# A cast moved between two groups of activations, and the last round of a convolution / recurrence loop rewoven

## The chip, the cores and the metric

The kernel runs on one core of a Trainium2 chip. The metric is device time in microseconds (us) for one execution. A core has five engines that run side by side, each with its own in-order queue: TensorE (PE in the profile; PEld is its weight load), VectorE (DVE), ScalarE (ACT), GpSimd (POOL) and SyncE (SP, which here issues nearly all DMA transfers). They wait for one another through semaphores.

## The reference

A two-layer generator backbone over 1024 latent tokens of width 1024 and 256 context tokens, in float32. The change lies in the first layer:

```python
z = h @ p["w_in"]
va, vg, ga, xb, gb = jnp.split(z, ...)             # each 1024 wide
# branch A
u = va * sigmoid(vg)
u = depthwise_conv(u, p["conv_w"], p["conv_b"])    # 31 taps along the tokens
y_a = silu(layernorm(u, ...)) * silu(ga)
# branch B, in both directions along the tokens
u = depthwise_conv(xb, p["sconv_w"], p["sconv_b"]) # 4 taps
r = sigmoid(u @ w_r + b_r); i = sigmoid(u @ w_i + b_i)   # per head of 128 channels
log_a = -8.0 * r * softplus(-lam); a = exp(log_a)
bx = sqrt(-expm1(2.0 * log_a)) * (i * u)
h[t] = a[t] * h[t-1] + bx[t]                       # context tokens first, then latent tokens
y_b = (h_forward + h_backward) * silu(gb)
out = concat([y_a, y_b]) @ p["w_out"]
```

The second layer (multi-scale pooling and a gate) and the final norm follow; the change does not touch them.

## The kernel before

Activations lie transposed: 128 channels on the partitions, tokens along the free dimension, in 8 channel tiles of 1024 tokens (1280 with context). A product in near float32 is made of three matmuls: every operand is split into a high part (`hi`, a cast on ScalarE, line 95) and a low part (`lo = x - hi`, a subtraction, line 96), and `mm3_steps` (line 119) adds hi·hi, hi·lo and lo·hi, 8 contraction steps for each half of 512 tokens. Weights are loaded by DMA and split in the same way by `wload` (line 107): ScalarE makes the high part, POOL the low part, in buffers that exist twice (`wr`, `wh`, `wl`).

**The rounds (lines 522 to 586).** One round for each channel tile j. A round
- takes the product `xb` (made in the round before), applies four taps and gives `uc`, then its high part `uh` (line 538, ScalarE) and its low part `ul` (line 571, VectorE);
- turns the gates of the tile before into decays (`decays`, line 441): for both directions a Tanh, then an Exp, then a Sqrt, in this order on ScalarE by explicit ordering (`issue_after`); the Sqrt's results are called `roots`;
- multiplies the `vg` weights (sigmoid on ScalarE, line 552, ordered behind the last root) and the `va` weights (line 561); VectorE multiplies both to `u` (line 564), which also frees the PSUM tile;
- runs the recurrence of the tile before (`recurrence`, line 460): two products on POOL (lines 463, 465), and for each direction on VectorE one combined product (line 468) and two scans (lines 475, 477); the sum of both directions is stored to DRAM as `yb_raw`;
- multiplies the four gate matrices of this tile (`gate_steps`, line 498, operands `uh` and `ul`), three pieces of tokens each, with a sigmoid on ScalarE (line 511). Between two such gate steps stand two steps of the next round's `xb` product (`weave`, line 515).

The last round has no next `xb`: there the gate steps alternate with the steps of the round's own `va` product:

```python
gws = wload(gw[j], f"gw{j}", nc.gpsimd, n=4 * P) if last else None
...
if last:
    weave(gate_steps(j, gws, (uh, ul), gates), value_steps(), 1)
```

**Behind the rounds.** Lines 716 to 730: for each j the product `gb` (line 722), its Silu (line 726), the product with the stored recurrence (`yr`, line 727), and its split into `ybh` and `ybl`. Then the 31 taps of the convolution, `conv_tap` (line 743), one VectorE instruction per tap and channel tile on a PSUM tile; the sum over channels and the layer norm (lines 771 to 785, the mean by a matmul `mu`, line 773); the output product `wob` of branch B (line 792); and the gate `ga` of branch A (lines 830 to 850), whose product with the normalised `u` is line 838.

**What sets the order.** The text is traced once, and a planner then orders the instructions of each engine by their place in the text and by planned times; a free engine takes the earliest instruction that is ready by the plan. So the taps, which are late in the text, fill VectorE's gaps from the first round on, and the order within each engine's queue is fixed when the kernel is built. `issue_after` adds an ordering on one engine; `high_priority(offset=EVAC)` lifts what empties PSUM. PSUM has four tiles for products (`psum`, 512 tokens) and two wide ones (`wide`: tag `cv` for the convolution, tag `xb` for the `xb` product and every second convolution tile).

Of the kernel before, what the change touches and what calls it, by code (L numbers as in the profile page):

```python
# [15 lines left out]
P = 128  # L16
# [39 lines left out]
def body(ctx, tc, xT, ctxT, cc, ccol, modT, modW, win, gw, wout, wu, grp, wg, wo1, small, edge, ident, outT):  # L56
# [52 lines left out]
    def wload(src, name, eng, n=D, out=None):  # L109
        raw = wpool.tile([P, n], F32, tag="wr", name=f"wr_{name}")  # L110
        load(raw, src)
        if out is None:
            hi = wpool.tile([P, n], F32R, tag="wh", name=f"wh_{name}")
            lo = wpool.tile([P, n], F32R, tag="wl", name=f"wl_{name}")
        else:
            hi, lo = out(f"wh_{name}", F32R), out(f"wl_{name}", F32R)
        split(raw, hi, lo, eng)
        return hi, lo
# [311 lines left out]
    with ExitStack() as actx:  # L430
# [9 lines left out]

        def decays(j, gates):
            rs, roots, last = gates[0::2], [], None

            def after(*args, **kw):
                nonlocal last
                with ExitStack() as octx:
                    if last is not None:
                        octx.enter_context(tc.issue_after(last.ins))
                    last = nc.scalar.activation(*args, **kw)  # L449

            for d in range(2):
                roots.append(ltile(f"th{j}_{d}"))
                after(roots[d], rs[d], AF.Tanh, scale=chalf[:, d * KT + j : d * KT + j + 1])
            for d in range(2):
                after(rs[d], rs[d], AF.Exp, scale=cneg[:, d * KT + j : d * KT + j + 1])
            for d in range(2):
                after(roots[d], roots[d], AF.Sqrt, bias=tiny)
            return roots, last

        def recurrence(j, uc, gates, roots):  # L460
            ats, ius = gates[0::2], gates[1::2]
# [4 lines left out]
            for d in range(2):  # L466
                iu, at = ius[d], ats[d]
                nc.vector.scalar_tensor_tensor(out=iu, in0=at, scalar=1.0, in1=iu, op0=add, op1=mult)
# [8 lines left out]
                nc.vector.tensor_tensor_scan(out=iu[:, lat], data0=at[:, lat], data1=iu[:, lat],  # L477
                                             initial=first, op0=mult, op1=add)
# [34 lines left out]


        def weave(some, others, n):
            for _ in some:
# [9 lines left out]
        for j in range(KT):  # L526
# [10 lines left out]
            uh, ul = utile(f"uh{j}", F32R), utile(f"ul{j}", F32R)  # L537
            nc.scalar.copy(uh, uc)
            taken = []

            roots, root = (None, None) if state is None else decays(j - 1, state[1])
            w = wload(win[KT + j], f"vg{j}", nc.gpsimd)
# [13 lines left out]
            us.append(u)  # L556
            gates, last = [], j == KT - 1

# [6 lines left out]

            gws = wload(gw[j], f"gw{j}", nc.gpsimd, n=4 * P) if last else None
            with ExitStack() as octx:
                if not last:
                    weave((), value_steps(), 1)
                    octx.enter_context(tc.issue_after(taken[0].ins))  # L570
                nc.vector.tensor_tensor(out=ul, in0=uc, in1=uh.bitcast(F32), op=sub)
# [143 lines left out]

    bh, bl = [], []
    for j in range(KT):
        w = wload(win[4 * KT + j], f"gb{j}", nc.gpsimd)
        th, tl = d2tile(f"ybh{j}", F32R), d2tile(f"ybl{j}", F32R)
        for h in range(2):  # L720
            ps = psum(f"gb{j}_{h}")
            mm3(ps, w, (hh, hl), HALF[h])
            y = vtile(f"yr{j}_{h}")
            nc.sync.dma_start(y, yb_raw[j][:, HALF[h]])
            sgt = ttile(f"sb{j}_{h}")
            nc.scalar.activation(sgt, ps, AF.Silu)
            nc.vector.tensor_tensor(out=y, in0=y, in1=sgt, op=mult)
            split(y, th[:, HALF[h]], tl[:, HALF[h]], nc.gpsimd)
        bh.append(th)
        bl.append(tl)  # L730
# [701 lines left out]
```

## Time and profile before

| | us |
|---|---|
| three runs | 1378.43, 1374.39, 1375.69 |
| their median | 1375.69 |
| the profiled execution, whole | 1381.07 |
| its span, first to last instruction | 1379.3 |

The mean granted clock of TensorE over the span is 0.974 of full speed. The profile is that of one execution; times of rows are counted from the first instruction. A row of the timeline has its start, its length, the engine, the line, the operation, the tile written and the tiles read, the shape, how many instructions are merged, and in brackets the idle time of the engine just before it and what ended it. A row of the list of waits has the waiting engine and line, what it waited for, the total, how often and the longest. A row of the busy time by stage has the stage, its length, each engine's busy time with its number of instructions, and the granted clock.

### The profile page before, as it was taken

The numbers are of one execution on the slowest core, as the hardware profiler recorded it, in microseconds if no ns is written. First come the engines' busy times: TensorE is split into PE (matmuls) and PEld (weight loads), VectorE is DVE, ScalarE is ACT, GpSimd is POOL, SyncE is SP. The second block draws the span as 40 slices with busy tenths as digits, with TensorE's granted clock in tenths as the row PEclk, the third lists the DMA queues.
The fourth block names the chain that finished last, engine by engine and source line by source line (L and its number), as shares of the span: only waits on it lengthen the run. The fifth ranks groups of instructions, "written<-read, shape, count | busy, mean of one in ns | idle before, by whom it ended". The sixth has DMA issues, their size and how long they took to land.

```text
span 1379.3 us, 15637 instructions
## 1 busy us (share of the span) xinstructions
PE 1295.9 (94%) x5664; PEld 1048.2 (76%) x5664; DVE 1205.1 (87%) x1587; ACT 632.7 (46%) x906; POOL 363.3 (26%) x182
## 2 busy tenths in 40 slices
PE   7889989898999799999998999999999999999896
PEld 4468868787777587787887887788888888778685
DVE  7998999999999999998778865999999987876775
ACT  6353644674465542304533544754334344634442
POOL 5173534743473555523320004000000000000002
PEclk9899999999999899999999999999999999999997
DMA  9753011111112113343353646424243334758623
GB/s 354 280 180 119 25 59 54 53 40 61 54 35 72 46 46 130 110 151 135 103 185 122 221 154 205 138 93 151 100 145 123 115 115 132 265 190 275 206 107 123
DMA packets 82866, 181.79 MB, mean 132 GB/s; under 512 B 7778, under 2 KB 27618, under 8 KB 82788
## 3 DMA queue, kind: packets, MB, share of 16 engines
q1 hardware_dynamic: 74340, 176.60, 37.8%
q10 hardware_dynamic: 8448, 4.20, 1.0%
q8 instruction: 44, 0.72, 0.2%
q14 instruction: 34, 0.28, 0.1%
HBM read 136.72 MB, written 44.04 MB: 131 GB/s over the span
## 4 chain that ended last, share of the span: by engine, by line
PE 36%; DVE 10%; DMA 7%; issue 2%; ACT 2%; POOL 1%; POOLq 0%; SPq 0%; DVEq 0%; ACTq 0%
PE ga L127 2%; PE ga L128 2%; PE ga L126 2%; PE wob L127 2%; PE wob L128 2%; PE wob L126 2%; DMA wr_g<-wg 1%; DVE ws L986 1%; DMA yr_t<-y_t 1%; DMA wr_v<-wfold 1%; PE qb_g L666 1%; DVE wq_g L96 1%; PE qb_g L669 1%; PE qb_g L668 1%; DVE wq_wo L96 1%
## 5 line engine op out<-in xcount | busy, mean ns | idle before, releaser
L746 DVE SCALAR_TENSOR_TENSOR conv<-u,sm,conv 128x1013 f32<-128x1013 f32 (+14 forms) x232 | 291.2, 1272 | 6.6 <-ACT conv L738 3.8
L1252 POOL TENSOR_TENSOR o<-x,rr 128x256 f32<-128x256 f32 (+1 forms) x9 | 8.0, 923 | 462.9 <-ACT rr L1240 460.0
L511 ACT ACTIVATE g<-g,sm 128x512 f32<-128x512 f32 (+1 forms) x96 | 58.8, 617 | 110.5 <-PE g L510 108.3
L96 POOL TENSOR_TENSOR wl_wu<-wr_wu,wh_wu 128x1024 fp32r<-128x1024 f32 x16 | 39.4, 2470 | 153.9 <-ACT wh_wu L95 147.7
L463 POOL TENSOR_TENSOR g<-g,uc 128x1280 f32<-128x1280 f32 x16 | 47.5, 2967 | 107.9 <-ACT g L511 65.1
L249 PE MATMUL fold<-gh,wh_wu 128*128 128x512 f32 x128 | 53.0, 416 | 5.7 <-ACT wh_wu L95 5.7
L250 PE MATMUL fold<-gl,wh_wu 128*128 128x512 f32 x128 | 52.4, 409 | 3.2 <-DVE gl L96 3.2
L128 PE MATMUL gb<-h0h,wl_gb 128*128 128x512 f32 x128 | 50.7, 398 | 4.8 <-POOL wl_gb L96 4.8
L126 PE MATMUL vg<-h0h,wh_vg 128*128 128x512 f32 x128 | 52.3, 408 | 2.7 <-ACT g L511 2.1
L251 PE MATMUL fold<-gh,wl_wu 128*128 128x512 f32 x128 | 50.7, 405 | 2.3 <-POOL wl_wu L96 2.3
L128 PE MATMUL xb<-h0h,wl_xb 128*128 128x512 f32 x128 | 50.2, 392 | 2.0 <-POOL wl_xb L96 2.0
L127 PE MATMUL wob<-ybl,wh_wob 128*128 128x512 f32 x128 | 50.5, 395 | 1.2 <-POOL ybl L96 1.2
L465 POOL TENSOR_TENSOR g<-g,th 128x1280 f32<-128x1280 f32 x16 | 46.9, 2948 | 16.8 <-ACT th L449 16.8
L127 PE MATMUL vg<-h0l,wh_vg 128*128 128x512 f32 x128 | 51.2, 400 | 0.0
L126 PE MATMUL gb<-h0h,wh_gb 128*128 128x512 f32 x128 | 50.6, 395 | 0.1
L126 PE MATMUL va<-h0h,wh_va 128*128 128x512 f32 x128 | 50.6, 395 | 0.0
L127 PE MATMUL va<-h0l,wh_va 128*128 128x512 f32 x128 | 50.6, 395 | 0.0
L508 PE MATMUL g<-uh,wh_gw 128*128 128x512 f32 (+1 forms) x96 | 36.3, 379 | 15.1 <-ACT wh_gw L95 6.4
L126 PE MATMUL wob<-ybh,wh_wob 128*128 128x512 f32 x128 | 50.6, 396 | 0.0
L128 PE MATMUL wob<-ybh,wl_wob 128*128 128x512 f32 x128 | 49.9, 391 | 0.7 <-POOL wl_wob L96 0.7
L128 PE MATMUL va<-h0h,wl_va 128*128 128x512 f32 x128 | 50.4, 395 | 0.0
L127 PE MATMUL gb<-h0l,wh_gb 128*128 128x512 f32 x128 | 50.4, 393 | 0.0
(548 smaller groups left out, 4301.1 us busy)
## 6 DMA issues: line engine op xcount, KB each, us to landing
mod<-modT SPq DMA_DIRECT2D x28, 512.0 KB, 5.5
wr_wu<-wu SPq DMA_DIRECT2D x16, 512.0 KB, 3.9
x_part<-xp SPq DMA_DIRECT2D x32, 256.0 KB, 2.4
mod<-modT SPq DMA_DIRECT2D x32, 256.0 KB, 3.3
wr_v<-wfold SPq DMA_DIRECT2D x16, 512.0 KB, 3.7
wr_g<-wg SPq DMA_DIRECT2D x16, 512.0 KB, 5.4
wr_wo<-wo SPq DMA_DIRECT2D x16, 512.0 KB, 4.2
yr_t<-y_t SPq DMA_DIRECT2D x16, 512.0 KB, 6.3
```

The lines of the kernel that those rows point to most:

```text
L96: eng.tensor_tensor(out=lo, in0=src, in1=hi.bitcast(F32), op=sub))
L126: nc.tensor.matmul(ps, hi[:, kc], xh[k][:, cols], start=(k == 0), stop=False)
L127: nc.tensor.matmul(ps, hi[:, kc], xl[k][:, cols], start=False, stop=False)
L128: nc.tensor.matmul(ps, lo[:, kc], xh[k][:, cols], start=False, stop=(k == ks - 1))
L249: nc.tensor.matmul(ps, wh[:, kc], gh[i], start=(i == 0), stop=False)
L250: nc.tensor.matmul(ps, wh[:, kc], gl[i], start=False, stop=False)
L251: nc.tensor.matmul(ps, wl[:, kc], gh[i], start=False, stop=(i == 3))
L463: nc.gpsimd.tensor_tensor(out=ius[d], in0=ius[d], in1=uc, op=mult)
L465: nc.gpsimd.tensor_tensor(out=ius[d], in0=ius[d], in1=roots[d], op=mult)
L508: nc.tensor.matmul(ps[:, :n], gwh[:, kc], uh[:, a : a + n], start=True, stop=False)
L511: nc.scalar.activation(t[:, a : a + n], ps[:, :n], AF.Sigmoid, bias=col(ob + d * KT + j))
L746: nc.vector.scalar_tensor_tensor(out=(us[j] if k == 30 else acp)[:, a:b], in0=us[j][:, a + o : b + o], scalar=col(O_CONVW + 31 * j + k), i ...
```

## The change

1. **`decays`** takes an optional pair `cast`; if it is given, the copy `uh <- uc` is put into the ordered series on ScalarE, between the two Exp and the two Sqrt. In the first round, which has no decays, the copy stays alone.
2. **`ul`** follows directly in the text, and no longer waits for the first value tile.
3. **`recurrence`** takes `ahead`: the second direction's product (line 468) is ordered on VectorE behind the second value product.
4. **The last round** loads its gate weights ahead of `vg`, into a buffer of the pool of `uc`, `uh` and `ul`; it makes `va` in one go like the other rounds, and its gate steps alternate, one for one, with the steps of the first `gb` product, which goes to a wide PSUM tile. The Silu of that product stands ahead of the last decays.
5. **The `gb` loop** starts with the second product and asks for each weight tile one tile ahead.
6. `wload` accepts two ready tiles as well as a function that gives them.

```diff
-        def decays(j, gates):
+        def decays(j, gates, cast=None):
 ...
-                    last = nc.scalar.activation(*args, **kw)
+                    last = f(*args, **kw)
 ...
             for d in range(2):
                 after(rs[d], rs[d], AF.Exp, scale=cneg[:, d * KT + j : d * KT + j + 1])
+            if cast is not None:
+                after(*cast, f=nc.scalar.copy)
             for d in range(2):
                 after(roots[d], roots[d], AF.Sqrt, bias=tiny)
 
-        def recurrence(j, uc, gates, roots):
+        def recurrence(j, uc, gates, roots, ahead=None):
 ...
-                nc.vector.scalar_tensor_tensor(out=iu, in0=at, scalar=1.0, in1=iu, op0=add, op1=mult)
+                with ExitStack() as octx:
+                    if d == 1 and ahead is not None:
+                        octx.enter_context(tc.issue_after(ahead.ins))
+                    nc.vector.scalar_tensor_tensor(out=iu, in0=at, scalar=1.0, in1=iu, op0=add, op1=mult)
 ...
+        def project_gate():
+            w = wload(win[4 * KT], "gb0", nc.gpsimd)
+            ps = wide("gb0", 1)
+            return ps, (x for h in range(2) for x in mm3_steps(ps[:, HALF[h]], w, (hh, hl), HALF[h]))
 ...
-            nc.scalar.copy(uh, uc)
+            last = j == KT - 1
             taken = []
-
-            roots, root = (None, None) if state is None else decays(j - 1, state[1])
+            if state is None:
+                nc.scalar.copy(uh, uc)
+                roots, root = None, None
+            else:
+                roots, root = decays(j - 1, state[1], (uh, uc))
+            nc.vector.tensor_tensor(out=ul, in0=uc, in1=uh.bitcast(F32), op=sub)
+            if last:
+                gws = utile(f"gw{j}", F32R)
+                gws = wload(gw[j], f"gw{j}", nc.gpsimd, n=4 * P, out=(gws[:, :H], gws[:, H : 2 * H]))
             w = wload(win[KT + j], f"vg{j}", nc.gpsimd)
 ...
-            gws = wload(gw[j], f"gw{j}", nc.gpsimd, n=4 * P) if last else None
-            with ExitStack() as octx:
-                if not last:
-                    weave((), value_steps(), 1)
-                    octx.enter_context(tc.issue_after(taken[0].ins))
-                nc.vector.tensor_tensor(out=ul, in0=uc, in1=uh.bitcast(F32), op=sub)
-            if last:
-                weave(gate_steps(j, gws, (uh, ul), gates), value_steps(), 1)
+            for _ in value_steps():
+                pass
 ...
-                recurrence(j - 1, *state, roots)
-            if not last:
+                recurrence(j - 1, *state, roots, taken[1])
+            if last:
+                gb0, steps = project_gate()
+            else:
                 xb, steps = project_xb(j + 1)
                 gws = wload(gw[j], f"gw{j}", nc.gpsimd, n=4 * P)
-                weave(gate_steps(j, gws, (uh, ul), gates), steps, 2)
+            weave(gate_steps(j, gws, (uh, ul), gates), steps, 1 if last else 2)
             state = uc, gates
+        sb0 = [ttile(f"sb0_{h}") for h in range(2)]
+        for h in range(2):
+            nc.scalar.activation(sb0[h], gb0[:, HALF[h]], AF.Silu)
         recurrence(KT - 1, *state, decays(KT - 1, state[1])[0])
 ...
     bh, bl = [], []
+    w_next = wload(win[4 * KT + 1], "gb1", nc.gpsimd)
     for j in range(KT):
-        w = wload(win[4 * KT + j], f"gb{j}", nc.gpsimd)
+        w = w_next
+        if 0 < j < KT - 1:
+            w_next = wload(win[4 * KT + j + 1], f"gb{j + 1}", nc.gpsimd)
         th, tl = d2tile(f"ybh{j}", F32R), d2tile(f"ybl{j}", F32R)
         for h in range(2):
-            ps = psum(f"gb{j}_{h}")
-            mm3(ps, w, (hh, hl), HALF[h])
+            if j == 0:
+                sgt = sb0[h]
+            else:
+                ps = psum(f"gb{j}_{h}")
+                mm3(ps, w, (hh, hl), HALF[h])
+                sgt = ttile(f"sb{j}_{h}")
+                nc.scalar.activation(sgt, ps, AF.Silu)
```

More of the change, by code (lines that the diff above doesn't have):

```diff
@@ L114, in wload @@
             lo = wpool.tile([P, n], F32R, tag="wl", name=f"wl_{name}")
+        elif callable(out):
+            hi, lo = out(f"wh_{name}", F32R), out(f"wl_{name}", F32R)
         else:
-            hi, lo = out(f"wh_{name}", F32R), out(f"wl_{name}", F32R)
+            hi, lo = out
         split(raw, hi, lo, eng)
@@ L438, in ltile, with after @@
             return lpool.tile([P, E], dt, tag="l", name=name)
-        def decays(j, gates):
+        def decays(j, gates, cast=None):
             rs, roots, last = gates[0::2], [], None
-            def after(*args, **kw):
+            def after(*args, f=nc.scalar.activation, **kw):
                 nonlocal last
@@ L556, in body @@
             us.append(u)
-            gates, last = [], j == KT - 1
+            gates = []
             def value_steps():
```

2 lines of the change are left out of this document (removed).

## The prediction

> **What bounds the kernel now.** I read the page first, then the chain of work that ended last, then busy time by stage, then who waited for whom inside the stage that the change touches.
>
> ```profile
> span 1379.3 us, 15637 instructions
> PE 1295.9 (94%) x5664; PEld 1048.2 (76%) x5664; DVE 1205.1 (87%) x1587; ACT 632.7 (46%) x906; POOL 363.3 (26%) x182
> ```
>
> TensorE looks like the bound, but a busy PE includes waiting in its pipeline. The chain, from 584 us on, is TensorE without a break, and the first thing on it that is not a `wob` product is the `mu` product of the layer norm:
>
> ```profile
> 584.05 0.50 PE wob L127
> 630.60 0.86 PE mu L773 x2
> ```
>
> The rounds, the `gb` branch and the convolution taps occupy 131 to 629 us:
>
> ```profile
> core 0: us, PE busy (x) PEld busy (x) DVE busy (x) ACT busy (x) POOL busy (x), PEclk, DMA share, GB/s
> 131.00:629.00 498.00, 464.67 (x2086) 380.69 (x2085) 481.99 (x396) 240.41 (x286) 236.81 (x100) 0.97 0.21 69
> 449.00:461.00 12.00, 5.88 (x14) 4.51 (x15) 10.04 (x8) 5.85 (x7) 7.63 (x3) 0.57 0.13 44
> ```
>
> This row decides the case. VectorE is busy 482.0 of 498 us, so it has 16.0 us of idle time in all. Its filler is the 31-tap convolution, which has no deadline inside the rounds but must be complete before `mu`:
>
> ```profile
> L746 DVE SCALAR_TENSOR_TENSOR conv<-u,sm,conv 128x1013 f32<-128x1013 f32 (+14 forms) x232 | 291.2, 1272 | 6.6 <-ACT conv L738 3.8
> ```
>
> So there are two clocks running side by side: TensorE through rounds, `gb` and `wob`, and VectorE through rounds and taps. They meet at `mu`:
>
> ```profile
> 627.95 1.28 DVE L758 TENSOR_TENSOR lnsum<-lnsum,u 128x512 f32<-128x512 f32 x2
> 631.50 9.66 DVE L776 TENSOR_TENSOR u<-u,mu 128x512 f32<-128x512 f32 x16 [1.60 <-PE mu L773]
> ```
>
> The sum over channels ends at 629.2 and `mu` runs at 630.6: today both arrive almost together. After `mu`, VectorE has the whole layer norm to do before it can consume the `ga` products, and TensorE has the rest of `wob` and the first `ga` tiles to do meanwhile. How much room that leaves:
>
> ```profile
> 680.78 1.29 DVE L838 TENSOR_TENSOR u<-u,ga 128x512 f32<-128x512 f32 x2 [0.74 <-ACT ga L836]
> 690.67 0.39 PE L128 MATMUL ga<-h0h,wl_ga 128*128 128x512 f32 x1
> 690.90 0.39 PE L126 MATMUL ga<-h0h,wh_ga 128*128 128x512 f32 x1
> ```
>
> Four PSUM tiles rotate. The second `ga` tile is consumed at 680.78 + 0.65 = 681.4; the sixth, which takes its place, starts at 690.9. TensorE could be 9.5 us earlier relative to VectorE here; beyond that it would stand still.
>
> **The change, part by part.** What TensorE loses today, up to 584 us:
>
> ```profile
> PE g L509 <- DVE ul L571: 6.7, 3, 3.0
> PE g L508 <- ACT wh_gw L95: 6.4, 1, 6.4
> PE g L508 <- DVE u L564: 6.2, 3, 2.3
> PE gb L128 <- POOL wl_gb L96: 4.8, 2, 3.3
> PE xb L128 <- POOL wl_xb L96: 2.0, 2, 1.6
> ```
>
> *TensorE.* `uh` moves ahead of the roots, and `ul` no longer waits for the first value tile, so the 6.7 us on `ul` go. The second direction's `L468` is put behind both value products on VectorE, so these free PSUM sooner and most of the 6.2 us go. In the last round the gate weights are loaded ahead of `vg`, and the value matmuls run first, which covers the 6.4 us. Of the 4.8 us on `wl_gb` I take half, since POOL's order decides it:
>
> ```profile
> 520.86 2.52 POOL L96 TENSOR_TENSOR ybl<-yr,ybh 128x512 fp32r<-128x512 f32 x2 [16.61 <-DMA yb_raw<-g]
> 525.74 0.79 PE L128 MATMUL gb<-h0h,wl_gb 128*128 128x512 f32 x1 [3.30 <-POOL wl_gb L96]
> ```
>
> POOL stood 16.6 us at the first `ybl` until the last recurrence was stored, with the low part of a `gb` weight behind it. Loading a tile ahead helps only where that low part comes before this wait in POOL's order. In all about 21 us. The half-clock stretches behind these waits go too: the stage ran at a mean clock of 0.97, 498 x 0.03 = 15 us lost, and the row 449 to 461 shows how: 0.57 of 12 us, behind the 6.4 us wait, is 5.2 us. Take two thirds of 15: 10. TensorE then reaches `mu` some 25 to 30 us earlier. Alternating the last gates with `gb0` adds no matmul; the matmuls are 0.23 us apart (690.67 and 690.90), so the 12 steps of three that lie between gates hold 8.2 us, and the last gate and with it the last recurrence come that much later in matmul count. Against the 6.4 us wait and its 5.2 us of half clock, that is even or better.
>
> *VectorE.* None of its instructions is removed, so only its waits and slow spots can shrink:
>
> ```profile
> DVE g L468 <- POOL g L465: 5.9, 4, 2.1
> DVE ul L571 <- ACT uh L538: 1.9, 1, 1.9
> DVE yr L727 <- ACT sb L726: 1.6, 1, 1.6
> L571 DVE TENSOR_TENSOR ul<-uc,uh 128x1280 fp32r<-128x1280 f32 x8 | 14.2, 1778 | 1.9 <-ACT uh L538 1.9
> 417.52 1.47 DVE L571 TENSOR_TENSOR ul<-uc,uh 128x1280 fp32r<-128x1280 f32 x1
> 490.73 3.37 DVE L727 TENSOR_TENSOR yr<-yr,sb 128x512 f32<-128x512 f32 x1 [1.59 <-ACT sb L726]
> 526.30 0.68 DVE L727 TENSOR_TENSOR yr<-yr,sb 128x512 f32<-128x512 f32 x1
> ```
>
> `ul` alone takes 1.47 us, its mean is 1.778: 8 x 0.31 = 2.5 us, plus the wait of 1.9, so 4.4 us if it falls where POOL is quiet. The first `yr` product waited 1.6 us for a Silu that now comes before the last decays: 1.6 us. The same product took 3.37 where another took 0.68; I give it half of the 2.7, 1.3 us (bounds 0 and 2.7).
>
> The other side is on ScalarE, and what waits for it:
>
> ```profile
> 397.41 2.62 ACT L449 ACTIVATE th<-th,tiny 128x1280 f32<-128x1280 f32 x2
> 401.35 0.60 ACT L552 ACTIVATE sg<-vg 128x512 f32<-128x512 f32 x1
> 401.84 1.26 ACT L538 CAST uh<-uc 128x1280 fp32r<-128x1280 f32 x1
> 398.92 5.86 POOL L465 TENSOR_TENSOR g<-g,th 128x1280 f32<-128x1280 f32 x2 [1.92 <-ACT th L449]
> 401.91 4.23 DVE L468 SCALAR_TENSOR_TENSOR g<-g,g 128x1280 f32<-128x1280 f32 x1 [1.83 <-POOL g L465]
> ```
>
> The cast (1.26 us, about 1.15 net of overlap) now stands between the exponentials and the roots. Roots, `sg`, POOL's `L465` and VectorE's first `L468` all stand behind it: each comes 1.15 us later in 7 rounds, 8.1 us in all. If `uc` is not finished, the cast and the roots wait for it as well. The cover is `ul` itself, 1.47 us of VectorE work that becomes ready in that gap; where it fills it, the cost is nothing. I take 0, bounds 0 and 8.1. The cast needs no table of its own: in the rows above it follows a sigmoid with no load between.
>
> The wait added to the second direction's `L468` (behind both value products) holds, in VectorE's order, its scans, the sum of both directions and the store of `yb`; the next round's decays take over those buffers.
>
> ```profile
> DVE u L564 <- PE va L128: 1.0, 1, 1.0
> ```
>
> VectorE has waited for a value product once in all rounds, in the first, for 1.0 us; taps stand ready to fill such a gap. I take nothing, bounds 0 and 1.0 per round.
>
> *At `mu`.* If TensorE arrives 25 us early it stands there, with the remaining `wob` tiles queued behind it, and resumes at half clock. By the row 449 to 461 that costs up to 5.2 us; one short stretch is a third of it, 1.7. I take 1.7.
>
> [...]
>
> *No cost on the path:* the new loader form; the last gate weights in the pool of `uc`, whose buffer comes free when POOL has used the previous `uc`, with TensorE on `vg` and `va` meanwhile; one or two table loads around the early Silu. On the SP queue the `gb` weights now stand ahead of the `yr` loads of the same tile; a load that waits for its buffer holds these back, but taps fill VectorE and TensorE has room.
>
> Sum on the path that ends last, VectorE up to `mu` and TensorE after it: -4.4 - 1.6 - 1.3 + 1.7 = **-5.6 us**. The profiled run took 1381.07 us (span 1379.3 plus 1.8 around it), so it would take 1375.5; the median of the runs is 1375.69, 5.4 below the profiled one, so **1370.1 us**.
>
> **Rivals.**
>
> *TensorE's gain gets through.* If the order written for TensorE has `mu` later among `wob` and `ga` tiles, up to 9.5 us more than VectorE's own savings arrives, and nothing is lost to half clock: -7.3 - 9.5 = -16.8 at most, 1359; half the room gives 1364. For it: TensorE has 25 us to give. Against it: the order is fixed at build time from planned times, in which contention and half clock need not appear, so `mu` may keep its place. Chance 0.17.
>
> *POOL's later product runs into the scans: slower.* VectorE and POOL slow one another when both work on SBUF:
>
> ```profile
> 456.76 1.48 DVE L468 SCALAR_TENSOR_TENSOR g<-g,g 128x1280 f32<-128x1280 f32 x1
> 408.91 4.48 DVE L477 TENSOR_TENSOR_SCAN g<-g,g 128x1024 f32<-128x1024 f32 x1
> 465.47 2.32 DVE L477 TENSOR_TENSOR_SCAN g<-g,g 128x1024 f32<-128x1024 f32 x1
> ```
>
> `L468` alone takes 1.48, beside POOL's `L465` 4.23; the scan 2.32 alone and 4.48 where POOL was late. Push `L465` back by 1.15 us in every round and the weight splits behind it land on the scan: 1.15 + 2.16 = 3.3 us per round. In five of seven rounds that is 16.5, less the savings of 7.3 and plus 1.7: +11, so 1387. In four it is +7.6, 1383. It decides from the third round on (9.9 - 7.3 + 1.7 = +4.3). Against it: `ul` fills part of the gap and the second direction is pushed later, where POOL is idle. Chance 0.20, mostly near the lower price.
>
> [...]
>
> *Nothing moves.* VectorE is full, its savings are eaten by the cast or by half clock: within 0.3%, 1376. Chance 0.13.
>
> **How the numbers follow.** The forecast has 0.50: its own spread (cast 0 to 8.1, value wait 0 to 7, `yr` 0 to 2.7, half clock 0 to 5.2) puts 0.33 of it beyond 0.3% and 0.17 within; 0.3% is 4.1 us, about what a measurement of this kernel can tell from no change. Faster: 0.33 + 0.17 = 0.50. Same: 0.17 + 0.13 = 0.30. Slower: 0.20. The range takes in the first rival's full room and the slower one's nearer price: 1358 to 1383.
>
> **What would show it.** Right: the waits for `ul`, `u` and `wh_gw` gone from TensorE's list; rounds shorter; a new wait of TensorE at `mu` or in the first `ga` tiles, 10 us or more; VectorE still busy 97% up to `mu`, which comes about 5 us earlier. Wrong on the fast side: `mu` waits for nobody and `ga` starts 10 us or more earlier. Wrong on the slow side: `L468`, `L475` and `L477` longer than their means now, or a longer wait for `L465`, with `mu` later than 630. The forecast fails altogether if VectorE's idle and slow spots move by more than 10 us for reasons that no row here shows.

## The result, and the profile after

The changed kernel takes **1393.32 us** (median of 4 runs, 1390.43 to 1394.86) against 1377.06 us for the kernel before in the same series: a ratio of 1.0123, 95% interval 1.0101 to 1.0144. It is 16 us slower where 5.6 us less was forecast, and lies above the range. The profiled execution of the changed kernel took 1390.43 us, its fastest; that of before, 1381.07 us, was 4 us above the median. So the two traces differ by 9 us where the medians differ by 16. Runs of one kernel lie up to 7 us to either side of their median: in what follows, sizes come from medians and places from traces.

First the head of the page after: span, and busy time by engine.

```profile
span 1388.6 us, 15640 instructions
PE 1299.9 (94%) x5664; PEld 1048.2 (75%) x5664; DVE 1211.8 (87%) x1587; ACT 637.6 (46%) x910; POOL 364.4 (26%) x182
```

The instructions are the same but for four more on ScalarE. VectorE's take 6.7 us longer in all (1205.1 us before); most of the loss is in waits. The timeline of the changed kernel, at the layer norm and at the first `ga` products:

```profile
641.77 2.78 DVE L784 TENSOR_TENSOR lnsum<-lnsum,u 128x512 f32<-128x512 f32 x1
...
690.77 1.27 DVE L864 TENSOR_TENSOR u<-u,ga 128x512 f32<-128x512 f32 x2
...
691.50 0.79 PE L128 MATMUL ga<-h0h,wh_ga 128*128 128x512 f32 x1 [3.73 <-DVE u L864]
```

The sum over channels ends at 644.6 us, 15 us later than before (629.2). VectorE then starts its `ga` products at 690.8 instead of 680.8, and TensorE, whose first `ga` matmul is on time (664.0 us, 663.5 before), stands 3.7 us in front of them. Of the two rows of busy time by stage below, the first is the whole stage of the prediction and the second the stretch around that wait (columns: length, busy time of TensorE, weight load, VectorE, ScalarE and POOL, granted clock, DMA share, GB/s):

```profile
131.00:629.00 498.00, 463.39 (x2078) 377.57 (x2078) 470.78 (x386) 242.27 (x287) 235.61 (x100) 0.97 0.21 69
...
689.00:697.00 8.00, 5.50 (x14) 4.35 (x15) 4.42 (x8) 8.00 (x9) 2.38 (x1) 0.57 0.07 6
```

VectorE, busy 482.0 us of the stage before, is busy 470.8: it lost 11 us to waiting and has that much work left at 629. Over the 8 us that take in the last 2.5 us of TensorE's wait and what follows it the granted clock is 0.57; the mean of the whole stage is 0.97 as before.

**Two clocks.** A clock means here the time at which one engine, if the other never held it, would bring the last `ga` matmul. All kernels have that matmul as a common point; from there to the end of the span lie 624 to 631 us in every trace. The tile view of before, of the changed kernel, and of the last experiment (which frees two resources) gives a kind of matmul, its count, its shortest, median and longest time in ns, and the first and last start in us:

```profile
L126 PE MATMUL ga<-h0h,wh_ga x128: 388/390/800, 663.5 to 750.3; 128*128 128x512 f32 x128
L128 PE MATMUL ga<-h0h,wl_ga x128: 388/390/398, 664.3 to 750.7; 128*128 128x512 f32 x128
L773 PE MATMUL mu<-lnsum,ones x4: 592/593/593, 630.4 to 632.0; 128*128 128x512 f32 x4
```

```profile
L128 PE MATMUL ga<-h0h,wh_ga x128: 387/389/799, 664.0 to 758.6; 128*128 128x512 f32 x128
L130 PE MATMUL ga<-h0h,wl_ga x128: 388/389/628, 664.5 to 759.0; 128*128 128x512 f32 x128
L799 PE MATMUL mu<-lnsum,ones x4: 590/592/592, 645.5 to 647.7; 128*128 128x512 f32 x4
```

```profile
L128 PE MATMUL ga<-h0h,wh_ga x128: 388/389/398, 652.1 to 739.3; 128*128 128x512 f32 x128
L130 PE MATMUL ga<-h0h,wl_ga x128: 388/389/396, 652.5 to 739.8; 128*128 128x512 f32 x128
L806 PE MATMUL mu<-lnsum,ones x4: 592/592/593, 625.8 to 627.4; 128*128 128x512 f32 x4
```

Where TensorE sets the pace, the last `ga` matmul starts 87.2 us after the first (750.7 - 663.5, before). Where VectorE sets it, it starts 113.5 us after `mu` (759.0 - 645.5, after). These two traces give the two constants; the others test them. The later of the two times meets the last `ga` matmul within 0.7 us in every trace except e2's, where both are close and it is 2 us too high. Some of them:

| kernel | first `ga` + 87.2 | `mu` + 113.5 | last `ga` in the trace |
|---|---|---|---|
| before | 750.7 | 743.9 | 750.7 |
| changed | 751.2 | **759.0** | 759.0 |
| changed, small `gb0` tiles (e3) | 751.8 | 750.7 | 752.3 |
| changed, start of the taps on VectorE (e8) | 759.5 | **770.2** | 770.5 |
| rounds' edits, free memory (e14) | 753.3 | 741.6 | 752.9 |
| changed, free memory (e16) | 747.5 | **755.2** | 755.8 |
| changed, small tiles, free memory (e18) | 739.3 | 739.3 | 739.8 |

Before, VectorE had 6.8 us of room. The change brings TensorE no earlier and VectorE 15 us later; 8.3 us of that shows. That places the 9 us between the two traces; the other 7 us between the medians are a matter of which execution was profiled, and no row here places them.

**Waits that went and came.** TensorE's list of waits after, 131 to 800 us:

```profile
PE gb L128 <- ACT wh_gb L95: 7.8, 2, 4.5
PE g L516 <- DVE uc L548: 7.1, 5, 4.1
...
PE ga L128 <- DVE u L864: 3.7, 1, 3.7
...
PE g L516 <- DVE u L585: 1.6, 3, 0.6
```

The waits for `ul` (6.7) and `wh_gw` (6.4) are gone and most of that for `u`; as much has come elsewhere. On VectorE, 131 to 700 us:

```profile
DVE conv L772 <- ACT conv L764: 9.1, 5, 4.4
DVE yr L753 <- ACT sb L605: 6.4, 1, 6.4
DVE g L476 <- POOL g L470: 5.9, 4, 1.8
```

The wait for the convolution's start has grown from 3.8 to 9.1, that for the first Silu from 1.6 to 6.4; that for POOL's product is what it was.

**The last round.** ScalarE's timeline after, in the last round. Line 519 is the gates' Sigmoid, line 605 the early Silu; line 452 is Tanh where it writes `th` from `g`, Exp where it reads `cneg`, and Sqrt where it reads `tiny`. A table load (`ACT_TABLE_LOAD`, 1.28 us each) is a row with no operands:

```profile
477.06 1.21 ACT L764 ACTIVATE conv<-u,sm 128x1024 f32<-128x1024 f32 x1 [6.68 <-DVE u L778]
478.21 1.03 ACT L519 ACTIVATE g<-g,sm 128x512 f32<-128x512 f32 x2
479.14 1.36 ACT L452 ACTIVATE th<-g,chalf 128x1280 f32<-128x1280 f32 x1
...
482.34 1.28 ACT L452 ACT_TABLE_LOAD   x1
483.64 1.37 ACT L452 ACTIVATE g<-g,cneg 128x1280 f32<-128x1280 f32 x1
485.02 1.28 ACT L519 ACT_TABLE_LOAD   x1
486.32 0.69 ACT L519 ACTIVATE g<-g,sm 128x512 f32<-128x512 f32 x1
487.03 1.28 ACT L452 ACT_TABLE_LOAD   x1
488.32 1.37 ACT L452 ACTIVATE g<-g,cneg 128x1280 f32<-128x1280 f32 x1
...
491.00 2.61 ACT L452 ACTIVATE th<-th,tiny 128x1280 f32<-128x1280 f32 x2
...
494.56 1.28 ACT L605 ACT_TABLE_LOAD   x1
495.86 1.08 ACT L605 ACTIVATE sb<-gb 128x512 f32<-128x512 f32 x2
...
497.31 1.22 ACT L764 ACTIVATE conv<-u,sm 128x1024 f32<-128x1024 f32 x1
```

Three things are to be seen. A convolution's start stands in ScalarE's queue in front of the gates' sigmoids and waits 6.7 us for the previous convolution on VectorE. The last sigmoid then falls between the two exponentials, with a table load of 1.28 us on either side of it (485.02 and 487.03). And the Silu called early runs at 495.9, behind everything; only then is the wide bank free, and the convolution that waits for it starts at 497.3. Before, that convolution started at 452.6, and the two exponentials stood side by side:

```profile
452.63 1.21 ACT L738 ACTIVATE conv<-u,sm 128x1024 f32<-128x1024 f32 x1
...
482.24 2.62 ACT L449 ACTIVATE g<-g,cneg 128x1280 f32<-128x1280 f32 x2
```

For 45 us VectorE had the taps of one convolution to fill its gaps with, instead of two.

**Behind the last recurrence.** After (POOL, then ScalarE):

```profile
525.60 2.54 POOL L96 TENSOR_TENSOR ybl<-yr,ybh 128x512 fp32r<-128x512 f32 x2 [8.69 <-DMA yb_raw<-g]
528.88 0.63 ACT L227 ACTIVATE cH<-cH 128x512 f32<-128x512 f32 x1 [12.98 <-DMA cH<-cc]
```

The first `ybl` belongs to tile 0, whose recurrence was stored long ago; still it waits for the store of the last one. The reason is memory, as e13 to e18 will show: the 16 buffers of `ybh` and `ybl` are laid over those of the rounds, and `ybl` of tile 0 got the buffer of the tile that the last recurrence stores. `cH`, a vector that VectorE first reads at 704 us, lies there too: its load is issued at 525.5, as that store ends.

### The profile page after: what moved, and what is told of

Same layout as the page of the kernel before. It is cut to its first block, busy times and chain, and to the rows that moved or that the text cites. A ratio compares the mean times of both kernels' runs of the same rounds, so it can differ in the third digit from the quotient of the medians.

```text
span 1388.6 us, 15640 instructions
## 1 busy us (share of the span) xinstructions
PE 1299.9 (94%) x5664; PEld 1048.2 (75%) x5664; DVE 1211.8 (87%) x1587; ACT 637.6 (46%) x910; POOL 364.4 (26%) x182
## 4 chain that ended last, share of the span: by engine, by line
PE 39%; DVE 38%; DMA 8%; ACT 6%; issue 6%; POOL 3%; SPq 0%; POOLq 0%; DVEq 0%; ACTq 0%
DVE conv L772 10%; DVE g L476 3%; DVE g L485 2%; DMA yr_t<-y_t 2%; PE wob L128 2%; PE wob L129 2%; PE wob L130 2%; PE fold L253 1%; PE fold L252 1%; PE fold L251 1%; DVE ws L1012 1%; DVE yr L753 1%; DVE uc L548 1%; DVE mod L834 1%; DMA mod<-modT 1%
## 5 line engine op out<-in xcount | busy, mean ns | idle before, releaser
L772 DVE SCALAR_TENSOR_TENSOR conv<-u,sm,conv 128x1021 f32<-128x1021 f32 (+14 forms) x232 | 292.9, 1271 | 11.9 <-ACT conv L764 9.1
L468 POOL TENSOR_TENSOR g<-g,uc 128x1280 f32<-128x1280 f32 x16 | 49.2, 3075 | 84.7 <-ACT g L519 48.3
L128 PE MATMUL ga<-h0h,wh_ga 128*128 128x512 f32 x128 | 51.7, 404 | 3.7 <-DVE u L864 3.7
L130 PE MATMUL vg<-h0h,wl_vg 128*128 128x512 f32 x128 | 50.3, 402 | 1.2 <-POOL wl_vg L96 1.2
L129 PE MATMUL ga<-h0l,wh_ga 128*128 128x512 f32 x128 | 50.8, 397 | 0.0
L130 PE MATMUL ga<-h0h,wl_ga 128*128 128x512 f32 x128 | 50.7, 396 | 0.0
```

Of the source, the lines that this page charges most:

```text
L128: nc.tensor.matmul(ps, hi[:, kc], xh[k][:, cols], start=(k == 0), stop=False)
L129: nc.tensor.matmul(ps, hi[:, kc], xl[k][:, cols], start=False, stop=False)
L130: nc.tensor.matmul(ps, lo[:, kc], xh[k][:, cols], start=False, stop=(k == ks - 1))
L468: nc.gpsimd.tensor_tensor(out=ius[d], in0=ius[d], in1=uc, op=mult)
L772: nc.vector.scalar_tensor_tensor(out=(us[j] if k == 30 else acp)[:, a:b], in0=us[j][:, a + o : b + o], scalar=col(O_CONVW + 31 * j + k), i ...
```

## The experiments

All medians in us; "before" is the kernel before in the same series. The theories in quotation marks are those of the expectations.

### e1 to e4: which half of the change?

e1 keeps the edits of the rounds (cast, `ul`, order of the second direction) and has the last round and the `gb` loop as before; e2 is the reverse. e3 and e4 are the changed kernel with one thing altered:

```diff
 e3
-            ps = wide("gb0", 1)
+                    ps.append(psum(f"gb0_{h}"))
 e4
-                roots, root = decays(j - 1, state[1], (uh, uc))
+            nc.scalar.copy(uh, uc)
+            roots, root = (None, None) if state is None else decays(j - 1, state[1])
```

> The edits of the rounds alone: cast of uh between the exponentials and the roots, ul right behind it, the second direction's L476 behind both value products. The last round and the gb loop stand as before the change. Theory 'last round' (the whole loss comes from gb0 in the wide bank, the convolution that starts late and the late Silu): no loss is left, 3 to 6 us faster than before. Theory 'cast' (the cast holds roots, sigmoids and the convolution's start on ScalarE in each of seven rounds): 8 to 12 us slower than before. Theory 'order' (any edit reshuffles the planned order, each a little worse): both halves slower, 5 to 8 us each.

> The edits of the last round alone: gates alternate with gb0, early gate weights, gb weights a tile ahead, early Silu. The cast, ul and the order of L476 stand as before the change. Theory 'last round': 12 to 16 us slower than before, with convolution 5 starting near 497 us and TensorE waiting 7 us or more on the high part of a gb weight. Theory 'cast': within 4 us of before, or faster. Theory 'order': 5 to 8 us slower.

> The changed kernel with gb0 in two PSUM tiles of 512 tokens, as the other gb products have them, in place of the wide bank that xb and the convolutions' projections take turns in. If the occupied bank is what costs in the last round: convolution 5 starts near 453 us as before the change instead of 497, and the kernel is 8 to 14 us faster than the changed one. If it is ScalarE's order (sigmoids behind the convolution's start, table loads) or the cast: within 3 us of the changed one.

> The changed kernel with the cast of uh as before the change: issued ahead of the decays and free of their order; ul still right behind. Theory 'cast': 5 us or more faster than the changed kernel. Theory 'last round': within 3 us of it.

| | this | before | ratio, interval |
|---|---|---|---|
| e1 rounds alone | 1387.75 | 1377.14 | 1.0062, 1.0040 to 1.0084 |
| e2 last round alone | 1382.49 | 1377.14 | 1.0037, 1.0020 to 1.0053 |
| e3 small `gb0` tiles | 1385.47 | 1377.14 | 1.0052, 1.0032 to 1.0071 |
| e4 cast free | 1393.94 | 1377.14 | 1.0108, 1.0090 to 1.0126 |

Both halves lose, 10.6 and 5.4, and the sum is the whole. The bank is worth 8 of the 16 us: in e3 the convolution that waited for it starts at 455.1 and `mu` comes at 637.2 instead of 645.5. So "last round" explained half; e2 by itself fits the numbers of "order". Theory "cast" had e4 faster by 5 us or more, and it is not. But e4 does not clear the cast, for it pays in another place, in a wait of VectorE that is 1.5 us in the changed kernel:

```profile
DVE ul L556 <- ACT uh L554: 13.1, 5, 4.7
```

How the rounds' edits lose shows in e1, ScalarE first, then POOL, ScalarE and TensorE:

```profile
485.15 0.60 ACT L742 ACTIVATE sb<-gb 128x512 f32<-128x512 f32 x1 [8.20 <-PE gb L130]
...
488.46 1.63 ACT L519 ACTIVATE g<-g,sm 128x256 f32<-128x256 f32 x3 [1.41 <-DVE g L485]
...
533.95 2.51 POOL L96 TENSOR_TENSOR ybl<-yr,ybh 128x512 fp32r<-128x512 f32 x2 [17.05 <-DMA yb_raw<-g]
537.17 0.63 ACT L227 ACTIVATE cH<-cH 128x512 f32<-128x512 f32 x1 [12.09 <-DMA cH<-cc]
540.85 0.79 PE L128 MATMUL gb<-h0h,wh_gb 128*128 128x512 f32 x1 [5.80 <-ACT sb L742]
```

Up to the eighth round TensorE is where it was (its `vg` products start at 436.3; 436.5 before). But the last three sigmoids run at 488.5, the last recurrence is stored 13 us later, ScalarE stands at `cH` with the `gb` Silus behind it, and TensorE runs out of PSUM.

### e5 to e8: which edit of the rounds, and does ScalarE hold the rest?

e5, e6 and e7 are the kernel before with one edit each: `ul` right behind the cast; the second direction's product behind the second value product; the cast between exponentials and roots. e8 is the changed kernel with

```diff
-        nc.scalar.activation(acp, us[j], AF.Identity, bias=col(O_CONVB + j), ...)
+        nc.vector.tensor_scalar(out=acp, in0=us[j], scalar1=col(O_CONVW + 31 * j + 15),
+                                scalar2=col(O_CONVB + j), op0=mult, op1=add)
```

> The kernel before with one edit: ul right behind the cast of uh, no longer behind the first value tile. The edits of the rounds together cost 0.6%, and the cast's place is not the reason in the changed kernel. Theory 'ul first' (1.5 us of VectorE work moves ahead of the convolution's end, whose successor starts on ScalarE in front of the gates' sigmoids): 5 to 10 us slower than before, with ScalarE's waits at the convolution's start near 9 and 7.5 us in place of 5.1 and 3.8. Theory 'order' (any edit reshuffles the planned order): 3 to 5 us slower, and the other two edits as much.

> The kernel before with one edit: the second direction's combined product ordered behind the second value product on VectorE. Theory 'ul first': within 3 us of before. Theory 'second direction late' (its scans and the store come later, and the next decays with them): 5 to 10 us slower. Theory 'order': 3 to 5 us slower.

> The kernel before with one edit: the cast of uh between the exponentials and the roots. Theory 'ul first' and theory 'second direction late': within 3 us of before. Theory 'order': 3 to 5 us slower. Should the cast cost something that the changed kernel hides, 8 us.

> The changed kernel with the convolution's first term (bias and middle tap) made by VectorE instead of ScalarE. No convolution start stands in ScalarE's order then, so it holds no sigmoid, Silu or cast; VectorE gets 8 instructions more, of about 1.2 us each by the taps of the same size, 9.6 us, and loses its own waits for that start (9.1 us). Theory 'ScalarE held by the convolution's start': TensorE's waits behind sigmoids, Silus and casts shrink by half or more, 6 us or more faster than the changed kernel. Theory 'VectorE alone sets the time': within 3 us of the changed kernel, or slower by up to 9.6.

| | this | before | ratio, interval |
|---|---|---|---|
| e5 `ul` alone | 1387.91 | 1376.51 | 1.0082, 1.0061 to 1.0103 |
| e6 order alone | 1382.10 | 1376.51 | 1.0042, 1.0026 to 1.0058 |
| e7 cast alone | 1383.53 | 1376.51 | 1.0053, 1.0036 to 1.0071 |
| e8 start on VectorE | 1400.43 | 1376.51 | 1.0168, 1.0143 to 1.0193 |

Each edit alone loses, and the three lose less together than apart: they lean on one another. The sign that e5's theory named, longer waits at the convolution's start, did not come (VectorE waits 3.8 us for it, as before). e5's are these, of VectorE and of TensorE:

```profile
DVE ul L556 <- ACT uh L554: 23.8, 7, 5.9
```

```profile
PE g L516 <- DVE u L579: 22.2, 6, 5.2
```

Without the cast moved forward, `ul` stands at the head of VectorE's queue and waits for `uh` behind the roots, and the value products that free PSUM wait behind `ul`. e7 is the cast without `ul`:

```profile
DVE g L470 <- POOL g L467: 13.0, 6, 3.3
```

That is 7.1 us more than the 5.9 of before, and the kernel is 7.0 us slower; the prediction put 8.1 us on an uncovered cast. That the one wait makes the whole loss is not shown: by the two clocks e7's later engine is TensorE, whose first `ga` matmul comes 6.5 us later than before (670.0). With `ul` beside the cast the same wait is 5.9 in the changed kernel, 9.0 in e1 and 7.4 in e18, so `ul` covers most of it. e6:

```profile
478.61 0.60 ACT L729 ACTIVATE sb<-gb 128x512 f32<-128x512 f32 x1 [7.80 <-PE gb L128]
...
481.70 1.63 ACT L514 ACTIVATE g<-g,sm 128x256 f32<-128x256 f32 x3 [1.19 <-DVE g L480]
```

In the old last round the value steps alternate with the gates, so "behind the second value product" is late there; the second scan and the buffer that the last gate takes over come late with it (the wait on the scan, line 480 of that kernel). A `gb` Silu planned ahead of these sigmoids holds ScalarE for 7.8 us; the wait that ends last is that for the scan. e8 refutes "ScalarE held by the convolution's start": ScalarE no longer makes that start, but TensorE's first `ga` matmul came 8.3 us later than in the changed kernel (672.3), `mu` at 656.7, and the kernel lost 7 us more. VectorE does not get eight instructions for nothing: the loss is within the 9.6 us that were expected for them.

### e9 to e12: the kernel before once more, and `cH`

e9 is the kernel before. e10 (rounds' edits) and e11 (changed, small tiles) order `cH`'s Silu behind the last `gb` Silu; e12 is e2 with small tiles.

```diff
-        nc.scalar.activation(t, t, AF.Silu)
+            if behind is not None:
+                octx.enter_context(tc.issue_after(behind.ins))
+            nc.scalar.activation(t, t, AF.Silu)
```

> The kernel before, unchanged, profiled once more. Its first profiled execution was 4 us above the median of its runs. Theory 'last recurrence' (the gb product ends 38.7 us after the Silu of the condition vector cH, which waits for the last recurrence's buffer with the gb Silus behind it on ScalarE; in the first profile cH came at 524.2 and left 7.4 us of slack): cH again near 524 and gb's end within 46 us of it; an execution near the median would show 3 to 5 us less half clock or waiting somewhere ahead of 663 us, not a shorter tail.

> The edits of the rounds alone (as in the first experiment), and the Silu of cH ordered on ScalarE behind the last gb Silu; cH is first read near 691 us. Theory 'last recurrence': TensorE's wait behind a gb Silu (5.8 us and the half clock after it) goes, gb ends 5 to 8 us earlier than the 576.1 of the rounds' edits alone, and the time falls by 5 to 10 us, back to within 4 us of before. Theory 'roots late' (what the rounds lose, they lose inside the rounds, by later roots and POOL products): within 3 us of the rounds' edits alone, 1387.8.

> The changed kernel with gb0 in two small PSUM tiles and the Silu of cH behind the last gb Silu. With small tiles alone gb ended at 572.9, 38.6 us after cH, and mu came at 637.2. Theory 'last recurrence': gb ends 4 us or more earlier, but ga is then held by VectorE, 113.6 us from mu to the last ga product: 1 to 3 us faster than small tiles alone (1385.5) by this bound, no more. Theory 'roots late': no change.

> The last round's edits alone (second experiment, 1382.5), with gb0 in two small PSUM tiles. If bank and rounds add up (16.2 = 10.6 for the rounds + 5.4 for the last round, and small tiles take 8 back): 1374 to 1377, no loss against before. If the small tiles only helped beside the rounds' edits: near 1382.

| | this | before | ratio, interval |
|---|---|---|---|
| e9 before again | 1375.50 | 1376.69 | 0.9997, 0.9981 to 1.0013 |
| e10 rounds, `cH` late | 1385.67 | 1376.69 | 1.0062, 1.0041 to 1.0084 |
| e11 small tiles, `cH` late | 1382.19 | 1376.69 | 1.0038, 1.0020 to 1.0056 |
| e12 last round, small tiles | 1384.84 | 1376.69 | 1.0053, 1.0033 to 1.0074 |

e9 repeats the distances of the first trace (the first `ybl` at 518.5 instead of 520.9, the end of `gb` 49.4 us behind it in both) and gives the resolution: 0.2%. e10 gained 2 us where 5 to 10 were expected: the next instruction that waits for the last recurrence has taken `cH`'s place. Its ScalarE:

```profile
541.53 0.62 ACT L95 CAST ybh<-yr 128x512 fp32r<-128x512 f32 x1 [14.43 <-DVE yr L746]
```

TensorE again waits 5.6 us for the `gb` Silu behind it. This `ybh` belongs to tile 1. By the code its `yr` takes one of two buffers, which come free when the first `ybl` is made, and that waits for the store. e11 came out 3.3 us under e3, near the bound of 1 to 3; its trace does not show why, since both `mu` and the last `ga` matmul are 1.4 us later there than in e3's. e12 refutes that bank and rounds add up (8 us above that expectation) and lies nearer the other one, 1382: with the rounds as before, TensorE is the later clock (last `ga` 754.9, `mu` + 113.5 = 747.7), so the bank brings it nothing.

### e13 to e16: the memory freed

Two pools of 8 buffers instead of one of 16; tiles 0 to 3 now lie on memory that is free early. `cH` stays late. e13 is before, e14 the rounds' edits, e15 the changed kernel with small tiles, e16 the changed kernel.

```diff
-    d2pool = ctx.enter_context(tc.tile_pool(name="d2pool", bufs=16, reuse_waits="tile"))
+    d2pools = [ctx.enter_context(tc.tile_pool(name=f"d2pool{i}", bufs=8, reuse_waits="tile")) for i in range(2)]
...
-        return d2pool.tile([P, S], dt, tag="d2", name=name)
+        d2count[0] += 1
+        return d2pools[(d2count[0] - 1) // 8 % 2].tile([P, S], dt, tag="d2", name=name)
```

> The kernel before with two edits. The 16 buffers for ybh and ybl come from two pools of 8 instead of one of 16, so that the tiles of branches 0 to 3 lie on memory that is free by then, and no longer on that of the last recurrence (ybl of tile 0 lay on the buffer whose store ends the last recurrence); and cH's Silu stands behind the last gb Silu. Theory 'buffers of the last recurrence': the 16.6 us of GpSimd at the first ybl and TensorE's 3.3 us at 525 us go, gb ends 3 to 6 us earlier, and since VectorE has 6.7 us of room at ga, the kernel is 3 to 6 us faster than before. Theory 'SP queue' (what stands behind the last store is held by the queue, whatever the memory): within 2 us of before.

> The edits of the rounds alone, with the same two edits. The rounds' edits alone ended gb at 576.1 us, 45.3 us after the last store, with a wait of 5.8 us behind a gb Silu and 6.8 us of half clock; cH alone brought nothing (1385.7), since the casts of ybh took its place. Theory 'buffers of the last recurrence': that wait goes, gb ends near 567, and the time falls 7 to 11 us from 1387.8, to 1377 to 1381. Theory 'roots late' (the loss lies inside the rounds): within 3 us of 1387.8.

> The changed kernel with gb0 in two small PSUM tiles and the same two edits. Theory 'buffers of the last recurrence': gb ends at 562 to 566 instead of 570 to 573; the end then hangs on VectorE, 113.6 us from mu (638 us) to the last ga product: 1380 to 1383, little under the 1382.2 with cH alone. If mu comes earlier as well (the products with the recurrence no longer stand in one heap behind the last store), 1374 to 1379.

> The changed kernel with the same two edits, gb0 still in the wide bank. There mu came at 645.5 and the last ga product 113.5 us later, while TensorE stood before the first of the ga products. Theory 'VectorE sets the end of the changed kernel through the bank': gb ends earlier but the time stays within 3 us of 1393.3. Theory 'buffers of the last recurrence' as the only cause: 7 to 11 us faster.

| | this | before | ratio, interval |
|---|---|---|---|
| e13 before, free memory | 1376.29 | 1377.13 | 0.9991, 0.9976 to 1.0007 |
| e14 rounds, free memory | 1380.47 | 1377.13 | 1.0015, 0.9995 to 1.0035 |
| e15 changed, small tiles, free memory | **1371.98** | 1377.13 | 0.9966, 0.9950 to 0.9983 |
| e16 changed, free memory | 1384.86 | 1377.13 | 1.0054, 1.0033 to 1.0074 |

The rounds' edits lose 7 of their 10.6 us of loss (e14, as expected, though `gb` ends at 572.6 and not near 567), and the changed kernel with both resources free beats the kernel before by 5 us.

Three expectations missed. The kernel before gains nothing from the memory: its `gb` ends at 570.2 as in its first trace. By the time alone that fits the theory "SP queue", but the trace refutes it, since GpSimd no longer waits for the last store, which is issued at 518.6:

```profile
496.73 2.53 POOL L96 TENSOR_TENSOR ybl<-yr,ybh 128x512 fp32r<-128x512 f32 x1
```

The wait went, and the end of `gb` did not move with it. e15 is faster than either of its two forecasts (1380 to 1383, and 1374 to 1379): `mu` comes at 626.0 where 638 was expected. And e16 gained 8.5 us where at most 3 was expected; its trace, the slowest of its runs, has `mu` 3.8 us earlier and the last `ga` matmul 3.2 us earlier, so 5 us of the gain have no place in it. The memory acts on VectorE as well, by a path that was not isolated.

### e17 and e18: what the rounds' edits are worth, and which of the two edits it was

e17 is e15 without the rounds' edits; e18 is e15 with `cH` as it was.

> The fastest version so far (changed kernel, gb0 in two small tiles, ybh and ybl on free memory, cH late: 1372.0) without the edits of the rounds: cast, ul and the order of the second direction's product as before the change. Theory 'the rounds' edits gain what was predicted once the last recurrence no longer holds gb': 3 to 6 us slower than 1372, near 1376. Theory 'all of the gain is the last round's': within 2 us of 1372. Theory 'roots late': faster, 1366 to 1370.

> The fastest version so far with cH's Silu where the planner puts it. If the memory alone carries the gain, within 2 us of 1372.0; if cH's Silu, which waits for the last recurrence's buffer in front of the gb Silus, holds gb by itself: 5 to 10 us slower, near the 1382 to 1385 of the small tiles alone.

| | this | before | ratio, interval |
|---|---|---|---|
| e17 e15 without the rounds' edits | 1381.39 | 1376.44 | 1.0042, 1.0029 to 1.0054 |
| e18 e15 with `cH` as it was | 1372.81 | 1376.44 | 0.9972, 0.9954 to 0.9989 |

The memory was it, not `cH` (0.8 us between e18 and e15). And the rounds' edits, which cost 10.6 us alone, are worth 9.4 us here (1381.39 - 1371.98), more than the 3 to 6 expected. "Order" as it was written, each edit a little worse, is refuted with that. That a part of the 9.4 us is a planned order that came out better by chance is not excluded. e18, POOL and VectorE:

```profile
500.31 2.87 POOL L96 TENSOR_TENSOR ybl<-yr,ybh 128x512 fp32r<-128x512 f32 x2
...
626.89 9.66 DVE L809 TENSOR_TENSOR u<-u,mu 128x512 f32<-128x512 f32 x16 [3.74 <-PE mu L806]
```

The first `ybl` waits for nothing and is 25 us earlier than in the changed kernel. VectorE waits at `mu` for TensorE, 4.6 us earlier than before; by the table above both clocks are level.

## Why the prediction was wrong

The step that failed is the paragraph *No cost on the path*. It put the early Silu, its table loads and the order of loads at nothing because "taps fill VectorE and TensorE has room", and two costs are not in it at all: the wide bank that the first `gb` product takes, and the memory behind the last recurrence.

- **The wide bank** was not looked up: who else takes it, and when. From 452 us on it is half of what fills VectorE's gaps. Held until 496 us it cost 8 us (e3).
- **The 16.6 us of POOL at the first `ybl`** were quoted, but only as something for a weight to be placed around. Why tile 0 should wait for tile 7 was not asked. In the changed kernel that memory, with `cH`'s place, cost 8.5 us (e16); bank and memory together cost 20.5 (1393.32 - 1372.81), more than the two apart, which fits an end set by the later of two clocks.
- **The path that ends last.** The sum counted VectorE's savings in full. By the two clocks TensorE was the later one before, with 6.8 us of room for VectorE; savings on VectorE alone would not have shown without an earlier TensorE.
- **VectorE's sum** came near the mark in a kernel in which neither resource binds (-5.6 predicted; -3.6 and -5.2 measured, e18 and e15), but that is luck. By the rows of e18 and of before, 131 to 626 us, `ul` gave 1.1 us of its 4.4 and the `yr` products 4.4 where 2.9 were counted; the scans gave 3.7 that no term had, and the wait for the convolution's start took 4.5 back. As built, the terms went the other way: the wait for the first Silu grew by 4.8 us instead of going, because that Silu ran behind the last decays; the wait of `ul` on `uh` fell by 0.4 of 1.9.
- **TensorE's 25 to 30 us** never came. `wob` started at 567.5 instead of 570.5, and even with both resources free at 562.4. A wait removed on TensorE came back on the next thing that a full VectorE, ScalarE or POOL owed it, and the mean clock of the stage stayed at 0.97. Adding up waits and half clock as if they were independent was wrong.
- **The 5.2 us of half clock** were read from a stretch, 449 to 461 us, that holds the wait itself. Behind the wait, from 454.4 us on, the clock is 0.50 for 3.6 us and 0.57 for 3.2, which loses some 3.2 us. The 1.7 us in the sum, a third of the 5.2, was the author's estimate, and no run shows it. Behind the 3.7 us wait of `ga` in the changed kernel the clock is 0.50 from 691.5 to 695.0 us and 0.74 from there to 698.0, which loses some 2.5 us.
- **The cast** at 0 with cover, 8.1 without: the sizes agree (5.9 us of wait in the changed kernel as before, 13.0 and 7.0 us of time without cover), though the cover was not full in e1 and e18, and e7's time hangs on TensorE.
- **The wait on the second value product** at 0: no such wait shows in the changed kernel's list. Alone the edit cost 5.6 us (e6), in a last round whose value steps alternate with the gates; the same change takes them out of there.
- **The slower rival**, POOL's product in the scans, did not happen. Groups of VectorE by line, of before and then of the changed kernel:

```profile
L477 DVE TENSOR_TENSOR_SCAN g<-g,g 128x1024 f32<-128x1024 f32 x16 | 40.7, 2543 | 0.0
L475 DVE TENSOR_TENSOR_SCAN g<-g,g 128x256 f32<-128x256 f32 x16 | 19.0, 1189 | 0.1
```

```profile
L485 DVE TENSOR_TENSOR_SCAN g<-g,g 128x1024 f32<-128x1024 f32 x16 | 39.7, 2479 | 0.0
L483 DVE TENSOR_TENSOR_SCAN g<-g,g 128x256 f32<-128x256 f32 x16 | 15.3, 958 | 0.0
```

The scans became shorter, and the wait for POOL's product stayed at 5.9 us. The kernel is slower, but not for the reason that "slower" was given its chance of 0.20.

Left open: how the memory moves `mu` in e16 and e15, and why e17, with the old rounds, stores its last recurrence 12.7 us later than e18 (533.6 and 520.9); its trace has three table loads more between 477 and 505 us, which is a part of it at most.

## What to carry to other kernels

Before costing a step at nothing, name for each buffer and bank that it takes who had it next, and from when. A long wait of an idle engine whose releaser makes no sense for the data (tile 0 waiting for tile 7) is memory handed on, and is worth finding even if nobody pays for it yet: it becomes the bound as soon as something else moves. Where two engines arrive together, work out both clocks to the next common point, and judge an edit by the later one; edits that each lose alone can gain together.

## What the runs showed of the hardware

In ScalarE's rows of the changed kernel, 478 to 496 us, a table load stands ahead of each Exp behind a Tanh or a Sigmoid (482.34, 487.03), of the Sigmoid behind an Exp (485.02), of the Sqrt behind an Exp (489.70) and of the Silu that comes next after the Sqrt and a cast (494.56). None stands ahead of the Tanh behind a Sigmoid (478.21 to 479.14). Each load takes 1.28 us, and the next activation starts 1.30 us after the load does (485.02 to 486.32); one activation, load and the next follow within 0.02 us. The one sigmoid between the two exponentials thus cost 2.6 us of loads on the path to the last recurrence.

The prediction has VectorE and POOL slow one another. In the trace of before, `ul` (line 571) took 1.47 us with POOL idle (417.52) and 2.89 beside it (452.76), and `L468` took 1.48 (460.52) and 4.23 (401.91); their operands are in SBUF by the code. A tap, which works on a PSUM tile, took 1.27 us with POOL idle (175.44) and 1.27 beside it (168.75). POOL's low part of a gate weight, 128x512, took 1.30 us where VectorE was mostly at a tap (224.13) and 3.28 where it was at a scan and at `L468` (411.20).
